# Rounded and rest passes of the side-by-side projections in runs instead of in turn, and some letters of the stage orders moved

## The chip, the cores and the metric

One core of one Trainium2 chip runs the whole program. The metric is the time of one execution on the device, in microseconds (us). Three runs of the kernel before gave 851.22, 853.45 and 853.88 us; their median, 853.45 us, is the time before. A separate execution was profiled: 852.3 us in all, of which 850.5 us lie between the first and the last instruction (the span).

The engines are named as in the profile: PE multiplies matrices (PEld is its loading of the stationary operand), ACT, DVE and POOL work on vectors, SP issues the transfers (DMA) of weights.

## The reference

A two-layer encoder of 256 tokens by 1024 channels, in float32, cut to what matters here:

```python
for i in range(2):
    h = rms_norm(x, norm_mix[i])
    x = x + (even_mixer if i == 0 else odd_mixer)(h, ...)   # Hyena + latent attention | differential attention
    x = x + cross_attention(rms_norm(x, norm_cross[i]), mem_n, xa_wq[i], xa_wkv[i], xa_wo[i])
    x = x + sq_relu_mlp(rms_norm(x, norm_mlp[i]), mlp_up[i], mlp_down[i])
return rms_norm(x, final_norm)
# cross_attention: q = h @ wq; k, v = split(mem_n @ wkv); 4 heads of 256, 256 memory tokens; softmax(q k^T) v @ wo
# sq_relu_mlp: square(relu(h @ w_up)) @ w_down, 1024 -> 4096 -> 1024
```

## The kernel before

PE takes float32 as it is (slowly) or in a rounded form, float32r. The kernel splits each operand into a rounded value and the rest that rounding left, both float32r: `weight` (lines 90 to 107) loads 512 KB of a weight into `wraw` by a DMA of SP's queue, ACT writes the rounded part `whi` and DVE the rest `wlo`. There are four `wraw` buffers and six pairs of `whi`/`wlo`, so ACT and DVE prepare weights ahead and then wait until PE gives a pair back. A product is three passes: rounded by rounded, rounded by rest, rest by rounded (`mm3`, lines 113 to 117).

For the queries of the cross-attention, the up-projections of the MLP and the keys of the first cross-attention the passes are laid side by side (`side_by_side`, line 223). The activations hold the rounded 256 tokens and the rests of the 256 tokens next to each other in one tile `both` (`t` in the rows, `memB` for the memory tokens). One matmul of 512 columns multiplies `whi` by both halves (line 229, here the rounded pass), and one of 256 columns adds `wlo` by the rounded half (line 225, here the rest pass). Both add into one PSUM bank of 512 columns; at the end `joined` (line 242) has ACT copy the second half and DVE add the first. Each pair of passes takes one 128 by 128 block of the weight. `proj_w4` (line 234) covers four banks of 128 output channels: the weight comes in four quarters, and a quarter holds two blocks for each bank, 8 pairs; a projection has 32. `mem_k2` (line 294) covers two banks with a weight in two halves of four blocks for each bank, 16 pairs. There are 4 query projections (two in each cross-attention), 16 up-projections and 4 key projections of the `mem_k2` kind. In each bank a rounded pass and its rest pass stand in turn; only in the last pair of a bank the rest comes first, so that the rounded pass ends the sum over the whole bank.

PSUM has eight banks, given out in turn by name: four `h`, three `b`, one `f`. A projection can write a bank only after ACT and DVE have read what stood in it.

The strings `ORDER_EVEN`, `ORDER_CROSS` and `ORDER_ODD` (lines 30 to 35) give the order in which the stages of a mixer or a cross-attention are written down; `run` (line 124) calls one function for each letter. A scheduler then merges the instructions of neighbouring stages into one fixed list for each engine, and each engine works through its list in order. In the cross-attention Q is the projection of two heads' queries, K keys, V values, S scores and softmax of a head, B the transposed probabilities times the values, W the output projection. In the even mixer G is the second layer of the filter features, R the transposed queries, S and O scores and outputs of a latent-attention head, F filters, T transposes to tokens, P the spectrum, W the first half of the output projection. In the odd mixer A is scores and softmax, B the product with the values and C the norm of a head.

`Gained` (line 185) transposes the residual as it comes out of the previous output projection and splits it for the next one; the last quarter of it is left over and done by `flush` after the first weight quarter of the next projection.

Of the kernel before, what the change touches and what calls it, by code (L numbers as in the profile page):

```python
# [17 lines left out]
P = 128  # L18
D = 1024
# [5 lines left out]
C1 = 6.28125  # L25
C2 = float(np.float32(TWO_PI - C1))
C3 = float(np.float32(TWO_PI - C1 - C2))
PI_LO = 3.1415925

ORDER_EVEN = "X J H0 L U K G R S0 D H1 F0 S1 T0 S2 S3 P0 O0 O1 O2 H2 S4 O3 H3 T1 F1 S5 S6 O4 O5 Y S7 H4 P1 H5 O6 O7 M W"  # L30
ORDER_CROSS = [
    "Q0 V0 K0 K1 S0 B0 K2 S1 Q1 K3 S2 W0 V2 B1 S3 B2 B3 W1",
    "K0 K1 Q0 V0 S0 S1 K2 B0 Q1 K3 S2 V1 B1 V2 B2 W0 V3 S3 B3 W1",
]
ORDER_ODD = "Q2 Q0 Q1 A0 A1 B0 A2 C0 B1 B2 Q4 C1 C2 Q3 A3 A4 Q5 A5 B3 B4 C3 A6 C4 B5 B6 C5 A7 W0 W1 C6 B7 C7"


@with_exitstack
def tile_encoder(ctx: ExitStack, tc: tile.TileContext, a: dict, out: bass.AP):
    nc = tc.nc  # L40
# [3 lines left out]
    def T(pool, shape, dt, tag, **kw):  # L44
        count[0] += 1
        return pool.tile(shape, dt, tag=tag, name=f"{tag}_{count[0]}", **kw)
# [10 lines left out]
    def hb():  # L57
        return T(ps, [P, 512], F32, "h", bufs=4)

    def wk():  # L60
        return T(ps, [P, 512], F32, "b", bufs=3)
# [7 lines left out]
    def hilo():  # L69
        z = t16().rearrange("p (k s n) -> p k s n", k=8, s=2)  # L70
        return z[:, :, 0, :], z[:, :, 1, :], z
# [10 lines left out]
    def h2(n=512):  # L82
        return T(ep, [P, 512], F32, "h2", bufs=8)[:, :n]
# [4 lines left out]
    def v3(t, k):  # L88
        return t.rearrange("p (k n) -> p k n", k=k)

    def weight(src, cols=1024, side=False, gi=None, nk=2, raw=None):
        p_, x, nr, nw = (rp, "f", 2, 2) if side else (wp, "w", 4, 6)
        if raw is None:
            raw = T(p_, [P, 1024], F32, x + "raw", bufs=nr)[:, :cols]
            nc.sync.dma_start(raw, src)
        hi = T(p_, [P, 1024], F32R, x + "hi", bufs=nw)[:, :cols]
        lo = T(p_, [P, 1024], F32R, x + "lo", bufs=nw)[:, :cols]
        if gi is None:
            split(hi, lo, raw)
            return hi, lo  # L100
        gi, k0 = gi
        for k in range(nk):
            g = gcol[:, gi, k0 + k:k0 + k + 1]
            h_, l_, r_ = (v3(z, nk)[:, k, :] for z in (hi, lo, raw))
            nc.scalar.activation(h_, r_, AF.Identity, bias=zero, scale=g)  # L105
            nc.vector.scalar_tensor_tensor(l_, r_, g, h_.bitcast(F32), op0=ALU.mult, op1=ALU.subtract)  # L106
        return hi, lo

    def split(hi, lo, src):
        nc.scalar.copy(hi, src)  # L110
        nc.vector.tensor_tensor(lo, src, hi.bitcast(F32), op=ALU.subtract)  # L111
# [12 lines left out]
    def run(order, **ops):  # L124
        for w in order.split():
            ops[w[0]](*(int(n) for n in w[1:]))
# [19 lines left out]
    h = hilo()[:2]  # L146
    lat_all = t16(F32)
    lat_raw = [lat_all[:, i * 832:(i + 1) * 832] for i in range(4)]
    for c in range(2):
        for t in range(2):  # L150
            cs = slice(c * 512, (c + 1) * 512)
# [68 lines left out]
            if mid is not None and q == at:  # L220
                mid()

    def side_by_side(b, w, both, kk):
        def low():
            nc.tensor.matmul(b[:, :256], w[1], both[:, kk, 0, :], start=False, stop=False)  # L225

        if kk == 7:
            low()
        nc.tensor.matmul(v3(b, 2), w[0], both[:, kk], start=kk == 0, stop=kk == 7)  # L229
        if kk < 7:  # L230
            low()

    def proj_w4(h, src, banks, gi, mid=None):
        both = h[2]
        for i in range(4):
            wh, wl = (v3(z, 2) for z in weight(src[i], gi=(gi, 2 * i)))
            for c in range(4):
                for k in range(2):
                    side_by_side(banks[c], [z[:, k, c * P:(c + 1) * P] for z in (wh, wl)], both, 2 * i + k)
            if mid is not None and i == 0:  # L240
                mid()

    def joined(b0, b1):
        y = v3(T(cur["jp"], [P, 512], F32, "join", bufs=3), 2)
        for i, b in enumerate((b0, b1)):
            nc.scalar.copy(y[:, i, :], b[:, 256:])
            nc.vector.tensor_tensor(y[:, i, :], b[:, :256], y[:, i, :], op=ALU.add)
        return y
# [35 lines left out]
    memB = T(cst, [P, 8, 2, 256], F32R, "memB")  # L284
# [9 lines left out]
    def mem_k2(l, u):  # L294
        bs = [wk(), wk()]
        for i in range(2):
            wh, wl = (v3(z, 4) for z in weight(a["xa_wk"][l, u, i]))
            for c in range(2):
                for k in range(4):
                    side_by_side(bs[c], [z[:, k, c * P:(c + 1) * P] for z in (wh, wl)], memB, 4 * i + k)  # L300
        y = joined(*bs)
        k = [T(rp, [P, 2, 256], F32R, f"kTm{i}", bufs=2) for i in range(2)]
        split(k[0], k[1], y)
        return k
# [177 lines left out]
    R = T(ep, [P, 256], F32, "rrow")  # L482
# [213 lines left out]
    def mla_proj():  # L696
        hs["b"] = [[wk(), wk()], [wk(), fl()]]
        proj_down(catm, (0, 1, 2, 3), a["w_out_ev"], (4, 5, 6, 7), hs["b"], True)

    run(ORDER_EVEN, S=mla_s, O=mla_o, H=hy_chunk, F=filters, T=toks, P=spec, Y=conv0, W=mla_proj, M=mem_T,  # L700
        J=lat_proj, L=latents, U=queries, K=keys_values, R=queries_T, D=tables, G=features_2, X=rope_gains)
    ys, banks = hs["y"], hs["b"]
    cat = hilo()[:2]
    for u in range(2):
        b = hb()
        b4 = b.rearrange("p (c t n) -> p c t n", c=2, t=2)
        for c in range(2):
            cs = slice((2 * u + c) * P, (2 * u + c + 1) * P)
# [3 lines left out]
        z = v3(h2(), 2)  # L712
# [12 lines left out]
    def cross(l, cur_):  # L725
# [11 lines left out]
        def qproj(u):  # L737
            bs = [hb() for _ in range(4)]
            proj_w4(h, a["xa_wq"][l, u], bs, 2 + l, lambda: cur_.flush(wk))
            for i in range(2):  # L740
                y = joined(*bs[2 * i:2 * i + 2])
                qTs[2 * u + i] = [v3(T(cur["jp"], [P, 512], F32R, "qT", bufs=8), 2) for _ in range(2)]
                split(*qTs[2 * u + i], y)
# [3 lines left out]
        def mk(hd):  # L747
            ks[hd] = mem_k(l, hd) if l else mem_k2(l, hd)
# [39 lines left out]
    def mlp(l, cur_, nxt):  # L788
# [10 lines left out]
        def up(f):  # L799
            uh = T(mp, [P, 4, 256], F32R, "uh", bufs=2)  # L800
            ul = T(mp, [P, 4, 256], F32R, "ul", bufs=2)
            bs = [hb() for _ in range(4)] if f == 0 else [wk(), wk(), wk(), fl()]
            proj_w4(h, a["mlp_up"][l, f], bs, 4 + l, lambda: cur_.flush(wk))
            if f == 1:
                banks.extend([hb(), hb()] for t in range(2))
            for j in range(2):
                y = joined(*bs[2 * j:2 * j + 2])
                sq = v3(t2(), 2)
                nc.vector.scalar_tensor_tensor(sq, y, 0.0, y, op0=ALU.max, op1=ALU.mult)
                split(uh[:, 2 * j:2 * j + 2, :], ul[:, 2 * j:2 * j + 2, :], sq)  # L810
            return uh, ul
# [36 lines left out]
    h, ssq = cur_.h, cur_.ssq  # L848
# [109 lines left out]

    run(ORDER_ODD, Q=qkv, A=od_a, B=od_b, C=od_c, W=od_out)
    nxt = Gained()  # L960
# [139 lines left out]
```

## Time and profile before

| | |
|---|---|
| runs | 851.22, 853.45, 853.88 us |
| profiled execution | 852.3 us, span 850.5 us |
| PE busy | 829.4 us, 98% of the span, 4514 matmuls |
| DVE, ACT, POOL busy | 586.6, 508.2, 19.5 us |
| moved by DMA | 138.89 MB, mean 163 GB/s |
| TensorE clock granted | 0.997 of full speed (mean) |

A matmul's duration in the profile contains time in which it lies over its neighbours (a matmul of 512 columns is given about 398 ns, while its successor starts 227 to 241 ns after it). What a matmul costs in a row of matmuls is therefore read from the distance of the starts, not from the duration. An idle time in brackets names the instruction that ended it.

### The profile page before, as it was taken

What the parts mean: (1) busy time and instruction counts of PE and PEld (TensorE: products, weight loads), DVE (VectorE), ACT (ScalarE), POOL (GpSimd) and SP (SyncE); (2) the same over time, 40 slices, a digit from 0 to 9 for tenths busy, and PEclk for the clock granted to TensorE, in tenths of its full rate; (3) what the DMA queues carried; (4) which work ended last, traced back from release to release, by engine and by line L of the source; (5) the groups of instructions that cost most, each with busy time, mean ns of one, the idle gap of its engine ahead of it and who ended that gap; (6) DMA issues with size and microseconds to landing.
All of it is one profiled execution on the core that took longest, in us unless ns stands there. A gap on an engine that the chain in (4) does not pass through costs nothing.

```text
span 850.5 us, 12079 instructions
## 1 busy us (share of the span) xinstructions
PE 829.4 (98%) x4514; PEld 695.0 (82%) x4514; DVE 586.6 (69%) x940; ACT 508.2 (60%) x883; POOL 19.5 (2%) x51
## 2 busy tenths in 40 slices
PE   6999999999999999999999999999999999999996
PEld 5867587788888888888888788889998888888885
DVE  4978796876658666666668888677654776666663
ACT  5896464766447555555567667666543755555542
POOL 0010000000000000000000010100000000000000
PEclk9999999999999999999999999999999999999998
DMA  7660317765527666666647416245522566656641
GB/s 275 199 207 19 121 36 263 236 209 159 170 68 218 202 187 190 192 191 186 196 132 226 153 66 198 75 145 178 159 90 100 168 201 189 189 191 184 191 125 50
DMA packets 39519, 138.89 MB, mean 163 GB/s; under 512 B 4515, under 2 KB 5155, under 8 KB 39461
## 3 DMA queue, kind: packets, MB, share of 16 engines
q1 hardware_dynamic: 39460, 138.13, 51.6%
q8 instruction: 35, 0.57, 0.3%
q14 instruction: 24, 0.19, 0.1%
HBM read 137.06 MB, written 1.05 MB: 162 GB/s over the span
## 4 chain that ended last, share of the span: by engine, by line
PE 79%; issue 11%; ACT 4%; DVE 2%; DMA 2%; POOL 1%; SPq 0%; POOLq 0%; ACTq 0%; DVEq 0%
PE h L115 12%; PE h L116 12%; PE h L117 12%; PE b L229 11%; PE b L225 5%; PE h L229 4%; PE f L229 3%; PE b L115 2%; PE h L225 2%; PE b L116 2%; PE b L117 2%; PE f L115 2%; PE f L116 2%; PE f L117 2%; PE f L225 2%
## 5 line engine op out<-in xcount | busy, mean ns | idle before, releaser
L111 DVE TENSOR_TENSOR wlo<-wraw,whi 128x1024 fp32r<-128x1024 f32 (+1 forms) x127 | 153.9, 1218 | 100.9 <-ACT whi L110 100.3
L110 ACT CAST whi<-wraw 128x1024 fp32r<-128x1024 f32 (+1 forms) x127 | 132.5, 1048 | 124.0 <-PE f L229 42.7
L105 ACT ACTIVATE whi<-wraw,zero,cpack 128x512 fp32r<-128x512 f32 x208 | 160.0, 811 | 62.6 <-PE h L117 20.3
L106 DVE SCALAR_TENSOR_TENSOR wlo<-wraw,cpack,whi 128x512 fp32r<-128x512 f32 x208 | 150.3, 749 | 42.8 <-ACT whi L105 42.6
L229 PE MATMUL b<-t,whi 128*128 128x512 f32 x336 | 119.5, 398 | 0.0
L117 PE MATMUL h<-whi,ul 128*128 128x512 f32 x256 | 99.9, 390 | 0.0
L115 PE MATMUL h<-whi,uh 128*128 128x512 f32 x256 | 99.6, 389 | 0.0
L116 PE MATMUL h<-wlo,uh 128*128 128x512 f32 x256 | 99.6, 389 | 0.0
L225 PE MATMUL b<-t,wlo 128*128 128x256 f32 x336 | 87.3, 280 | 0.0
L115 PE MATMUL h<-whi,t 128*128 128x512 f32 x192 | 76.8, 401 | 0.0
L116 PE MATMUL h<-wlo,t 128*128 128x512 f32 x192 | 76.5, 399 | 0.0
L117 PE MATMUL h<-whi,t 128*128 128x512 f32 x192 | 76.0, 397 | 0.0
L229 PEld LDWEIGHTS b<-t,whi 128*128 128x128 f32 x336 | 61.1, 188 | 12.2
L229 PE MATMUL h<-t,whi 128*128 128x512 f32 x192 | 67.9, 400 | 1.4 <-DVE t L111 1.4
L225 PEld LDWEIGHTS b<-t,wlo 128*128 128x128 f32 x336 | 63.4, 189 | 3.7
L116 PEld LDWEIGHTS h<-wlo,uh 128*128 128x128 f32 x256 | 48.0, 188 | 10.1
L117 PEld LDWEIGHTS h<-whi,ul 128*128 128x128 f32 x256 | 48.1, 188 | 9.9
L115 PEld LDWEIGHTS h<-whi,uh 128*128 128x128 f32 x256 | 48.1, 188 | 9.3
L225 PE MATMUL h<-t,wlo 128*128 128x256 f32 x192 | 50.0, 281 | 0.0
L229 PE MATMUL f<-t,whi 128*128 128x512 f32 x112 | 42.7, 398 | 0.0
L117 PEld LDWEIGHTS h<-whi,t 128*128 128x128 f32 x192 | 36.1, 188 | 7.2 <-DVE t L111 0.2
L115 PEld LDWEIGHTS h<-whi,t 128*128 128x128 f32 x192 | 36.1, 188 | 7.0
(325 smaller groups left out, 1633.1 us busy)
## 6 DMA issues: line engine op xcount, KB each, us to landing
wraw<-in_mlp_up_dram SPq DMA_DIRECT2D x64, 512.0 KB, 4.2
wraw<-in_mlp_down_dram SPq DMA_DIRECT2D x64, 512.0 KB, 4.3
wraw<-in_od_w_qkv_dram SPq DMA_DIRECT2D x24, 512.0 KB, 4.3
wraw<-in_xa_wq_dram SPq DMA_DIRECT2D x16, 512.0 KB, 4.1
wraw<-in_xa_wo_dram SPq DMA_DIRECT2D x16, 512.0 KB, 4.2
wraw<-in_w_hy_dram SPq DMA_DIRECT2D x12, 512.0 KB, 4.0
wraw<-in_w_out_ev_dram SPq DMA_DIRECT2D x8, 512.0 KB, 4.4
wraw<-in_xa_wv_dram SPq DMA_DIRECT2D x8, 512.0 KB, 5.4
```

What stands on the lines that cost most here:

```text
L105: nc.scalar.activation(h_, r_, AF.Identity, bias=zero, scale=g)
L106: nc.vector.scalar_tensor_tensor(l_, r_, g, h_.bitcast(F32), op0=ALU.mult, op1=ALU.subtract)
L110: nc.scalar.copy(hi, src)
L111: nc.vector.tensor_tensor(lo, src, hi.bitcast(F32), op=ALU.subtract)
L115: nc.tensor.matmul(o, lh, rh, start=first, stop=False)
L116: nc.tensor.matmul(o, lh, rl, start=False, stop=False)
L117: return nc.tensor.matmul(o, ll, rh, start=False, stop=last)
L225: nc.tensor.matmul(b[:, :256], w[1], both[:, kk, 0, :], start=False, stop=False)
L229: nc.tensor.matmul(v3(b, 2), w[0], both[:, kk], start=kk == 0, stop=kk == 7)
```

## The change

The diff, cut to its core (two orders of three are left out here: in the even mixer G moves from before R to behind S0, P0 and S3 change places, and so do S5 and S6; in the odd mixer A5 and B3 change places, and B5 and B6):

```diff
 ORDER_CROSS = [
-    "Q0 V0 K0 K1 S0 B0 K2 S1 Q1 K3 S2 W0 V2 B1 S3 B2 B3 W1",
+    "Q0 V0 K0 K2 S0 K1 B0 V2 S1 Q1 K3 S2 B1 W0 S3 B2 B3 W1",
...
-    def side_by_side(b, w, both, kk):
...
+    def side_by_side(banks, w, both, k0):
+        wh, wl = w
+        nk = wh.shape[1]
+        last = k0 + nk == 8
+
+        def high(c, k):
+            nc.tensor.matmul(v3(banks[c], 2), wh[:, k, c * P:(c + 1) * P], both[:, k0 + k],
+                             start=k0 + k == 0, stop=last and k == nk - 1)
+
+        def low(c, k):
+            nc.tensor.matmul(banks[c][:, :256], wl[:, k, c * P:(c + 1) * P], both[:, k0 + k, 0, :],
+                             start=False, stop=False)
+
+        every = range(len(banks))
+        for cs in [(c,) for c in every] if last else [every]:
+            for one in (low, high) if k0 // nk % 2 else (high, low):
+                for c in cs:
+                    for k in range(nk):
+                        one(c, k)
...
     def proj_w4(h, src, banks, gi, mid=None):
-        both = h[2]
         for i in range(4):
-            wh, wl = (v3(z, 2) for z in weight(src[i], gi=(gi, 2 * i)))
-            for c in range(4):
-                for k in range(2):
-                    side_by_side(banks[c], [z[:, k, c * P:(c + 1) * P] for z in (wh, wl)], both, 2 * i + k)
+            w = [v3(z, 2) for z in weight(src[i], gi=(gi, 2 * i))]
+            side_by_side(banks, w, h[2], 2 * i)
             if mid is not None and i == 0:
                 mid()
```

A four-bank projection now does its first quarter as 8 rounded passes over all banks and then 8 rest passes, the second as 8 rests and 8 rounded, the third as 8 rounded and 8 rests, and the last bank by bank, two rests and two rounded each. With the neighbours joined that is a run of 8, runs of 16, 16 and 8, and then runs of 2. A two-bank key projection has 8 rounded, 8 rests, and then bank by bank four rests and four rounded. No matmul is added or taken away; line 229 keeps its number for the rounded pass, and the rest pass is now line 233.

PE, the first query projection of the first cross-attention, before (`h_1503` to `h_1506` are its four banks, `whi_1509` and `wlo_1510` its first weight quarter, `t_297` the activations, `b_1531` the bank of `flush`):

```order
L229 MATMUL h_1503<-t_297_1388,whi_1509 128x512
L225 MATMUL h_1503<-t_297_1388,wlo_1510 128x256
...
L229 MATMUL h_1504<-t_297_1388,whi_1509 128x512
L225 MATMUL h_1504<-t_297_1388,wlo_1510 128x256
...
L229 MATMUL h_1506<-t_297_1388,whi_1509 128x512
L225 MATMUL h_1506<-t_297_1388,wlo_1510 128x256
...
L181 MATMUL b_1531<-cpack_70,t_296_1385 128x128 x4
L229 MATMUL h_1503<-t_297_1388,whi_1540 128x512
```

The same place on PE after the change:

```order
L229 MATMUL h_1503<-t_297_1388,whi_1509 128x512 x2
L229 MATMUL h_1504<-t_297_1388,whi_1509 128x512 x2
L229 MATMUL h_1505<-t_297_1388,whi_1509 128x512 x2
L229 MATMUL h_1506<-t_297_1388,whi_1509 128x512 x2
L233 MATMUL h_1503<-t_297_1388,wlo_1510 128x256 x2
L233 MATMUL h_1504<-t_297_1388,wlo_1510 128x256 x2
L233 MATMUL h_1505<-t_297_1388,wlo_1510 128x256 x2
L233 MATMUL h_1506<-t_297_1388,wlo_1510 128x256 x2
L181 MATMUL b_1531<-cpack_70,t_296_1385 128x128 x4
L233 MATMUL h_1503<-t_297_1388,wlo_1541 128x256 x2
```

The fourth bank, written first after 12 passes of both kinds before, is now written after 6 rounded ones.

PE, the first key projection (K0) of the first cross-attention, before, with the last row of the values (V0) ahead of it (`b_1708` and `b_1709` are the two banks of K0, `b_1629` one of V0):

```order
L117 MATMUL b_1629<-whi_1686,memB_91 128x512
L229 MATMUL b_1708<-memB_91,whi_1712 128x512
L225 MATMUL b_1708<-memB_91,wlo_1713 128x256
...
L229 MATMUL b_1709<-memB_91,whi_1712 128x512
L225 MATMUL b_1709<-memB_91,wlo_1713 128x256
```

The same place on PE after the change:

```order
L117 MATMUL b_1629<-whi_1686,memB_91 128x512
L229 MATMUL b_1708<-memB_91,whi_1712 128x512 x4
L229 MATMUL b_1709<-memB_91,whi_1712 128x512 x4
L233 MATMUL b_1708<-memB_91,wlo_1713 128x256 x4
L233 MATMUL b_1709<-memB_91,wlo_1713 128x256 x4
L233 MATMUL b_1708<-memB_91,wlo_1735 128x256 x4
```

The second bank follows four rounded passes now, where four rounded and four rest passes stood ahead of it.

PE, the transposed probabilities of head 1 (L455, a part of B1) in the first cross-attention, before (`b_2183` is a bank of the values V2, `b_2271` the bank of B1's product, `b_2286` that of the scores S3):

```order
L117 MATMUL b_2183<-whi_2240,memB_91 128x512
L455 MATMUL b_2264<-cpack_70,t_401_1937 128x128 x4
L115 MATMUL b_2271<-t_468_2262,vp_355_1702 128x256
L115 MATMUL b_2286<-kTm_435_2114,qT_2059 128x256
L116 MATMUL b_2286<-kTm_436_2115,qT_2059 128x256
```

The same step on PE after the change (L459 are the transposes, `b_2231` is the bank of the product, `h_2246` and `h_2247` are banks of W0):

```order
L117 MATMUL b_2198<-kTm_378_1815,qT_2131 128x256
L459 MATMUL b_2224<-cpack_70,t_417_2017 128x128 x4
L115 MATMUL h_2246<-whi_2252,t_317_1499 128x512
...
L116 MATMUL h_2247<-wlo_2259,t_317_1499 128x512
L115 MATMUL b_2231<-t_458_2222,vp_355_1702 128x256
```

Between the transposes and the product that uses them stand 17 matmuls of the output projection W0; before, nothing stood there. V2 stands behind B0's transposes and ahead of S1.

## Rows read from the trace of the kernel before

**Rows 1.** The page: busy time; granted clock in 40 slices; chain that ended last.

```profile
PE 829.4 (98%) x4514; PEld 695.0 (82%) x4514; DVE 586.6 (69%) x940; ACT 508.2 (60%) x883; POOL 19.5 (2%) x51
...
PEclk9999999999999999999999999999999999999998
...
PE 79%; issue 11%; ACT 4%; DVE 2%; DMA 2%; POOL 1%; SPq 0%; POOLq 0%; ACTq 0%; DVEq 0%
```

**Rows 2.** Groups by line and shape, line 229 (columns as page part 5).

```profile
L229 PE MATMUL b<-t,whi 128*128 128x512 f32 x336 | 119.5, 398 | 0.0
...
L229 PE MATMUL h<-t,whi 128*128 128x512 f32 x192 | 67.9, 400 | 1.4 <-DVE t L111 1.4
...
L229 PE MATMUL f<-t,whi 128*128 128x512 f32 x112 | 42.7, 398 | 0.0
...
L229 PE MATMUL b<-memB,whi 128*128 128x512 f32 x64 | 22.6, 398 | 0.1
```

**Rows 3.** Timeline of PE, one up-projection: start, duration in us, then engine and instruction.

```profile
698.77 0.39 PE L229 MATMUL b<-t,whi 128*128 128x512 f32 x1
...
707.25 0.40 PE L229 MATMUL b<-t,whi 128*128 128x512 f32 x1
...
710.04 0.39 PE L115 MATMUL h<-whi,uh 128*128 128x512 f32 x1
```

**Rows 4.** Timeline, end of V0: first and last of 14 matmuls of 512 columns.

```profile
168.62 0.39 PE L116 MATMUL b<-wlo,memB 128*128 128x512 f32 x1
...
171.57 0.39 PE L117 MATMUL b<-whi,memB 128*128 128x512 f32 x1
```

**Rows 5.** Timeline, second-layer keys: first and last of 48 matmuls of 256 columns.

```profile
565.90 0.28 PE L115 MATMUL f<-memB,fhi 128*128 128x256 f32 x1
...
571.54 0.28 PE L117 MATMUL f<-memB,flo 128*128 128x256 f32 x1
```

**Rows 6.** Timeline, first query projection: what its third quarter waits for.

```profile
147.83 0.39 PE L229 MATMUL h<-t,whi 128*128 128x512 f32 x1
...
149.15 0.68 DVE L111 TENSOR_TENSOR t<-h,t 128x512 fp32r<-128x512 f32 x1
...
153.27 0.57 ACT L110 CAST t<-b 128x512 fp32r<-128x512 f32 x1
...
155.23 0.49 PE L229 MATMUL h<-t,whi 128*128 128x512 f32 x1 [1.12 <-DVE t L111]
```

**Rows 7.** Timeline, K0: first pass, DVE reading V0's banks, second bank.

```profile
171.79 0.39 PE L229 MATMUL b<-memB,whi 128*128 128x512 f32 x1
...
172.69 1.28 DVE L111 TENSOR_TENSOR vp<-b,vp 128x512 fp32r<-128x512 f32 x2
...
173.43 0.50 PE L229 MATMUL b<-memB,whi 128*128 128x512 f32 x1
```

**Rows 8.** Timeline, B1 of the first cross-attention.

```profile
228.79 0.60 PE L455 MATMUL b<-cpack,t 128*128 128x128 f32 x4
...
229.47 0.59 ACT L110 CAST t<-b 128x512 fp32r<-128x512 f32 x1
...
230.12 0.39 PE L115 MATMUL b<-t,vp 128*128 128x256 f32 x1 [0.73 <-ACT t L110]
```

**Rows 9.** Timeline, end of the odd mixer and start of the second cross-attention's queries.

```profile
563.13 0.28 PE L117 MATMUL f<-memB,flo 128*128 128x256 f32 x1
...
563.68 0.50 PE L229 MATMUL h<-t,whi 128*128 128x512 f32 x1 [0.28 <-DVE t L111]
```

**Rows 10.** Timeline, the latent attention's part of the even output projection.

```profile
124.98 0.50 PE L116 MATMUL f<-wlo,catm 128*128 128x512 f32 x1 [0.75 <-DVE wlo L111]
```

**Rows 11.** Timeline, start of the second layer's first up-projection.

```profile
664.95 0.40 PE L229 MATMUL h<-t,whi 128*128 128x512 f32 x1
...
665.15 0.69 DVE L278 TENSOR_TENSOR t<-h,t 128x512 f32<-128x512 f32 x1 [0.39 <-PE h L117]
```

**Rows 12.** Timeline, even mixer: PE's first filter matmuls.

```profile
51.32 3.67 PE L385 MATMUL h<-t,aT 128*128 128x512 f32 x8
```

More of the change, by code (lines that the diff above doesn't have):

```diff
@@ L28 @@
 PI_LO = 3.1415925
-ORDER_EVEN = "X J H0 L U K G R S0 D H1 F0 S1 T0 S2 S3 P0 O0 O1 O2 H2 S4 O3 H3 T1 F1 S5 S6 O4 O5 Y S7 H4 P1 H5 O6 O7 M W"
+ORDER_EVEN = "X J H0 L U K R S0 G D H1 F0 S1 T0 S2 P0 S3 O0 O1 O2 H2 S4 O3 H3 T1 F1 S6 S5 O4 O5 Y S7 H4 P1 H5 O6 O7 M W"
 ORDER_CROSS = [
-    "Q0 V0 K0 K1 S0 B0 K2 S1 Q1 K3 S2 W0 V2 B1 S3 B2 B3 W1",
+    "Q0 V0 K0 K2 S0 K1 B0 V2 S1 Q1 K3 S2 B1 W0 S3 B2 B3 W1",
     "K0 K1 Q0 V0 S0 S1 K2 B0 Q1 K3 S2 V1 B1 V2 B2 W0 V3 S3 B3 W1",
 ]
-ORDER_ODD = "Q2 Q0 Q1 A0 A1 B0 A2 C0 B1 B2 Q4 C1 C2 Q3 A3 A4 Q5 A5 B3 B4 C3 A6 C4 B5 B6 C5 A7 W0 W1 C6 B7 C7"
+ORDER_ODD = "Q2 Q0 Q1 A0 A1 B0 A2 C0 B1 B2 Q4 C1 C2 Q3 A3 A4 Q5 B3 A5 B4 C3 A6 C4 B6 B5 C5 A7 W0 W1 C6 B7 C7"
 @with_exitstack
@@ L221, in proj_xs @@
                 mid()
-    def side_by_side(b, w, both, kk):
[L224 to L231, printed above, removed]
+    def side_by_side(banks, w, both, k0):
[14 more added lines that the diff above has]
+                        one(c, k)
     def proj_w4(h, src, banks, gi, mid=None):
-        both = h[2]
         for i in range(4):
-            wh, wl = (v3(z, 2) for z in weight(src[i], gi=(gi, 2 * i)))
-            for c in range(4):
-                for k in range(2):
-                    side_by_side(banks[c], [z[:, k, c * P:(c + 1) * P] for z in (wh, wl)], both, 2 * i + k)
+            w = [v3(z, 2) for z in weight(src[i], gi=(gi, 2 * i))]
+            side_by_side(banks, w, h[2], 2 * i)
             if mid is not None and i == 0:
@@ L296, in mem_k2 @@
         for i in range(2):
[L297 to L300, printed above, removed]
+            side_by_side(bs, [v3(z, 4) for z in weight(a["xa_wk"][l, u, i])], memB, 4 * i)
         y = joined(*bs)
```

## The prediction

> **What bounds the kernel now.** I read the page first: PE is busy for 829.4 of 850.5 us, and the chain that ended last is PE for 79% and "issue" for 11% (an engine waiting for nothing that the profile shows); ACT, DVE and DMA together hold 8% [rows 1]. So the time is the sum of the distances between the starts of PE's matmuls, and only two things can change it: that distance, and PE's few waits. Next I read the grouped lines for how many matmuls the edit touches: line 229 has 336, 192, 112 and 64 matmuls [rows 2], together 704 rounded passes, each with one rest pass. Then the timeline for their distances, and last the timeline around PE's waits.
>
> **The pace of passes in turn and in runs.** In an up-projection the first three weight quarters are 24 pairs in turn. They take from 698.77 to 707.25 us, 8.48 us, that is 353.3 ns a pair; the last quarter, where the order is rounded, rest, rest, rounded, takes from 707.25 to 710.04 us for 8 pairs, 348.8 ns a pair [rows 3]. So the distance depends on what stands next to what: with two changes of kind for each pair it is 353.3, with one 348.8. For runs of one kind the nearest rows are other matmuls of the same shapes: 512 columns follow each other every 226.9 ns (168.62 to 171.57 us, 13 steps) [rows 4], 256 columns every 120.0 ns (565.90 to 571.54 us, 47 steps) [rows 5]. A pair in runs would then cost 346.9 ns, 6.4 ns less than in turn.
>
> How many pairs gain: the last quarter of a four-bank projection has two rests and two rounded passes in turn after the change as well, so it gains nothing. The other 24 pairs go into runs, in 20 such projections 480. Of the 16 pairs in each of the four two-bank key projections I count 12, since their second half keeps runs of only four; 48 more. 528 times 6.4 ns is 3.4 us. Three changes of kind remain in the first three quarters; at half of the 6.4 ns each, 20 x 3 x 3.2 ns, they take back 0.2. The term is **-3.2 us**.
>
> Its bounds: if runs get no further than the two-and-two order of the last quarter (348.8), 528 x 4.5 ns is 2.4 us. If every change of kind costs 4.5 ns, as the step from 353.3 to 348.8 would have it, a pair without any costs 344.3: 528 x 9.0 less 60 x 4.5 ns is 4.5 us. I take 6.4, because its two rows are long runs of exactly these shapes.
>
> The granted clock doesn't enter: it stood at the upper of its two levels, 2.4 GHz, in all slices but the last [rows 1].
>
> The Trainium skill ("TensorE: Matmul & The Clock Gate", section "Back-to-back issue gap") gives a distance of columns through 2.4 GHz plus about 2.5 ns, whatever stands ahead. By it, as an estimate, a pair would cost 325 ns in either order, and this term would be zero. The trace disagrees, since 8 pairs take different times in two orders [rows 3]; what would happen if the order didn't matter is the second rival below.
>
> **The first query projection.** Its third quarter starts at 155.23 after a wait of 1.12 us for the split of the part that `flush` transposes; ACT begins that split only at 153.27, behind other work of its list [rows 6]. ACT's list has the same order there after the change, so what PE gains in the first two quarters (16 pairs, 0.1 us) is waited away: **+0.1**. The fourth bank is now wanted after 6 rounded passes, 1.4 us after the start, where 6 pairs took 2.1 us before; DVE still reads it until 149.83 [rows 6], 2.0 us after the start at 147.83. That stall of some 0.6 us also falls into the 1.12 us and costs nothing as long as that wait stands; without this cover it would cost 0.6. Behind PE's wait stand flush's transposes, which ACT doesn't want before 153.27.
>
> **K0.** PE starts it at 171.79; its second bank is one that V0 filled, and DVE reads it in the first of two operations from 172.69 on; PE got it at 173.43 [rows 7]. By then all 8 passes into the first bank were done. Now only four rounded ones stand ahead (0.9 us, until 172.70), and PE waits about 0.7 us in place of 0.2. The four rests (4 x 0.12) that used to fill the time come later: **+0.45**. Below that it can be nothing, if DVE is there earlier; above, 0.7.
>
> The same earlier wish for a bank arises in every projection. The nearest row for the rest is the second layer's first up-projection: start 664.95, DVE's last reading from 665.15 for 0.69, so until 665.84; the fourth bank is wanted at 664.95 + 1.36 = 666.31 [rows 11]. There 0.5 us remain, so I count nothing; between two up-projections a whole down-projection lies.
>
> **B1 of the first cross-attention.** PE's transposes start at 228.79 and take 0.44; then PE waits for ACT, which begins its copy at 229.47, and goes on at 230.12 [rows 8]: 0.9 us with nothing between. After the change 17 matmuls of W0 stand there, 17 x 0.227 = 3.9 us, which covers ACT's 0.59 and DVE's split. V2 now stands ahead of S1, and B0's product is covered by 8 rounded passes of the next query projection (1.8 us). **-0.9**; at worst none, if B0's transposes now wait in its stead.
>
> **End of the odd mixer.** From 563.13 to 563.68 PE stands for 0.55 us where 0.12 would do, for DVE's split ahead of the second cross-attention's queries [rows 9]. After the change 25 matmuls of the second layer's keys and values stand between (25 x 0.12 = 3.0 us). **-0.4**. The wait moves nowhere else that I see: those matmuls were due anyway.
>
> **The even mixer.** Its letters move several things of about one us. For gain: the rest of a weight for which PE waits 0.75 us until 124.98 [rows 10] stood in DVE's list behind four splits of the memory tokens; it now stands ahead of them, and the wait could go. For loss: the queries' copies now come ahead of G's sine on ACT, and PE's first filter matmuls, which began at 51.32 [rows 12], now stand ahead of the scores of head 1 and want G's result some 1.5 us earlier; S0 follows right on the transposes whose copies it needs. I bound this part by -0.75 (the one wait gone, nothing new) and +1.5 (the wait stays and the filters stand for those 1.5 us), and take **0**, since the wait that may go and one that may come are of the same order and no row tells which is the larger.
>
> **Sum.** -3.2 + 0.1 + 0.45 - 0.9 - 0.4 + 0 = -3.95 us on the profiled 852.3, which gives 848.35, a factor of 0.9954. The profiled execution lies 0.13% below the median of the runs shown, so on 853.45 it is **849.5 us**.
>
> **Rivals.**
> 1. The runs pay more, and the even mixer's wait goes: -4.5 for the pace instead of -3.2, and -0.75: 849.5 - 2.05 = 847.4. For it: the step between the two orders in rows 3. Against: rows 4 and 5 show 346.9 in runs that have no change of kind at all.
> 2. The pace doesn't follow the order. Then only the waits move: 0.45 - 0.9 - 0.4 = -0.85, so 852.6, no change. For it: rows 4 and 5 are of other operands than these passes. Against: rows 3. The page of the Trainium skill cited above speaks for this one. A variant: the pace is won, but the mixers give 1.5 us and B1's 0.9 back, 851.9.
> 3. Slower: the banks. A run of 8 rounded passes wants the last bank 0.7 us earlier in all 24 projections. If ACT and DVE had just been in time in the others, as in K0 (0.5 us lost), 20 more times 0.5 is 10 us against the 3.2 won: 859.5. It decides from about 12 such projections on. For it: K0 and the first query projection in rows 6 and 7. Against: 0.5 us to spare in rows 11, and banks that lie idle for a whole down-projection.
>
> **How the numbers follow.** 0.3% of the median is 2.6 us, about what can be told from no change; faster is below 850.9, slower above 856.0. The forecast has 0.55, with a range of its own of 847.8 to 851.2; rival 1 has 0.15; rival 2 with its variant 0.23; rival 3 has 0.07. Of the forecast 0.51 lies below 850.9; with rival 1 faster gets 0.66. Same gets 0.04 + 0.23 = 0.27, slower 0.07. The range leaves out rival 3 and the ends of the others: 846.5 to 852.8.
>
> **What would show it.** In the trace after, an up-projection from its first rounded pass to the first matmul of the down-projection should take 11.1 us in place of 11.27 [rows 3]; rounded passes in a run 227 ns apart, rests 120. K0 should stand about 0.7 us ahead of its second bank. No wait should follow the transposes of B1, and the second cross-attention's queries should start without one. PE's waits in the even mixer should sum to what they were. It would be wrong if rounded passes in a run stood 233 ns or more apart, if PE stood in many projections after the sixth rounded pass, or if the first cross-attention began more than 1.5 us later than before.

## The result, and the profile after

Four runs of the kernel after gave 846.05 to 846.86 us, median 846.43; four of the kernel before beside them 853.66. The ratio is 0.9921, with a 95% interval from 0.9904 to 0.9938: 6.7 us less (5.3 to 8.2). The forecast was 849.5, a gain of 4.0 us. The sign was right. The median lies 0.07 us below the range of 846.5 to 852.8; by the ratio, on the 853.45 us that the forecast started from, the time is 846.7 us, just inside it. The gain is 1.7 times the forecast, and, as the experiments show, its largest single part comes from the even mixer, which the forecast had at 0. Further runs of the kernel before, beside the experiments, have medians of 852.98 to 853.16.

The page of the kernel after; its span is 844.7 us, its time 846.44:

```profile
PE 824.9 (98%) x4514; PEld 695.0 (82%) x4514; DVE 589.7 (70%) x940; ACT 511.1 (61%) x883; POOL 19.3 (2%) x51
...
PEclk9999999999999999999999999999999999999998
...
PE 81%; issue 11%; ACT 4%; DVE 1%; POOL 1%; DMA 0%; SPq 0%; POOLq 0%; ACTq 0%; DVEq 0%
```

PE still bounds it: the same 4514 matmuls at the same clock [rows 1], 4.5 us less busy. ACT, DVE and DMA hold 5% of the chain instead of 8.

The groups of line 229 after, by shape:

```profile
L229 PE MATMUL b<-t,whi 128*128 128x512 f32 x336 | 90.7, 392 | 0.0
...
L229 PE MATMUL h<-t,whi 128*128 128x512 f32 x192 | 50.9, 394 | 0.4 <-DVE t L111 0.4
...
L229 PE MATMUL f<-t,whi 128*128 128x512 f32 x112 | 34.6, 390 | 0.0
L229 PE MATMUL b<-memB,whi 128*128 128x512 f32 x64 | 16.6, 394 | 0.0
```

A lesson in reading: against [rows 2] the busy sums fall by 60 us in all, though the kernel gained 7. The time in which passes of one group lie over each other is counted once: in a run neighbours are of one group, in turn they belong to two. Only distances of starts tell the pace. The idle time ahead of the queries fell from 1.4 to 0.4 us.

An up-projection after, at the place of [rows 3] (x6 stands for six passes in one row): start, end of the third quarter, first matmul of the down-projection:

```profile
693.77 1.52 PE L229 MATMUL b<-t,whi 128*128 128x512 f32 x6
...
702.10 0.40 PE L233 MATMUL b<-t,wlo 128*128 128x256 f32 x2
...
704.89 0.39 PE L115 MATMUL h<-whi,uh 128*128 128x512 f32 x1
```

24 pairs take 8.33 us where they took 8.48, and the whole 11.12 instead of 11.27. The rounded passes of a run stand 227 ns apart, the rests 120, as in [rows 4, 5].

K0 after, at the place of [rows 7]: first passes on PE, DVE reading V0's banks:

```profile
169.74 2.08 PE L229 MATMUL b<-memB,whi 128*128 128x512 f32 x8
```
```profile
169.88 1.37 DVE L111 TENSOR_TENSOR vp<-b,vp 128x512 fp32r<-128x512 f32 x2 [0.31 <-ACT vp L110]
```

DVE reads the banks 0.14 us after K0's start, not 0.90 as before; PE gets the second bank with a delay of 0.1. The forecast stall of 0.7 is not there.

B1 after, at the place of [rows 8]: ACT's copy of the transposes, and the first product:

```profile
224.54 0.58 ACT L110 CAST t<-b 128x512 fp32r<-128x512 f32 x1
...
225.18 0.39 PE L115 MATMUL b<-t,vp 128*128 128x256 f32 x1
```

No wait is left. Nor has the second cross-attention's first query pass one [rows 9]:

```profile
564.98 1.32 PE L229 MATMUL h<-t,whi 128*128 128x512 f32 x5
```

The wait of [rows 10] in the even output projection is gone as well, while others grew, among them this one ahead of the filters, where there was none [rows 12]. It is a wait for a load and not, as the prediction had it, for G's result. The query projection's wait of [rows 6] shrank to 0.42 us:

```profile
49.84 1.52 PE L389 MATMUL h<-t,aT 128*128 128x512 f32 x3 [0.79 <-DMA t<-in_hy_w_dram]
```
```profile
153.15 2.14 PE L229 MATMUL h<-t,whi 128*128 128x512 f32 x8 [0.42 <-DVE t L111]
```

### The profile page after: what moved, and what is told of

Read it like the earlier page. It is cut to its first block, busy times and chain, and to the rows that moved or that the text cites. A ratio compares the mean times of both kernels' runs of the same rounds, so it can differ in the third digit from the quotient of the medians.

```text
span 844.7 us, 12071 instructions
## 1 busy us (share of the span) xinstructions
PE 824.9 (98%) x4514; PEld 695.0 (82%) x4514; DVE 589.7 (70%) x940; ACT 511.1 (61%) x883; POOL 19.3 (2%) x51
## 2 busy tenths in 40 slices
DMA packets 39518, 138.89 MB, mean 164 GB/s; under 512 B 4514, under 2 KB 5154, under 8 KB 39460
## 4 chain that ended last, share of the span: by engine, by line
PE 81%; issue 11%; ACT 4%; DVE 1%; POOL 1%; DMA 0%; SPq 0%; POOLq 0%; ACTq 0%; DVEq 0%
PE h L115 12%; PE h L117 12%; PE h L116 12%; PE b L229 11%; PE b L233 6%; PE h L229 5%; PE f L229 3%; PE b L115 3%; PE b L116 3%; PE b L117 3%; PE h L233 2%; PE f L115 2%; PE f L116 2%; PE f L117 2%; PE f L233 2%
## 5 line engine op out<-in xcount | busy, mean ns | idle before, releaser
L105 ACT ACTIVATE whi<-wraw,zero,cpack 128x512 fp32r<-128x512 f32 x208 | 158.3, 810 | 54.0 <-PE h L117 20.8
L229 PE MATMUL b<-t,whi 128*128 128x512 f32 x336 | 90.7, 392 | 0.0
L229 PEld LDWEIGHTS b<-t,whi 128*128 128x128 f32 x336 | 59.3, 189 | 9.0
L233 PEld LDWEIGHTS b<-t,wlo 128*128 128x128 f32 x336 | 49.8, 190 | 4.7
L233 PE MATMUL b<-t,wlo 128*128 128x256 f32 x336 | 53.5, 282 | 0.0
L229 PE MATMUL h<-t,whi 128*128 128x512 f32 x192 | 50.9, 394 | 0.4 <-DVE t L111 0.4
L116 PEld LDWEIGHTS h<-wlo,t 128*128 128x128 f32 x192 | 36.1, 188 | 6.7
L229 PEld LDWEIGHTS h<-t,whi 128*128 128x128 f32 x192 | 33.6, 188 | 6.3 <-DVE t L111 1.3
```

What stands on the lines that cost most here:

```text
L116: nc.tensor.matmul(o, lh, rl, start=False, stop=False)
L229: nc.tensor.matmul(v3(banks[c], 2), wh[:, k, c * P:(c + 1) * P], both[:, k0 + k], start=k0 + k == 0, stop=last and k == nk - 1)
L233: nc.tensor.matmul(banks[c][:, :256], wl[:, k, c * P:(c + 1) * P], both[:, k0 + k, 0, :], start=False, stop=False)
```

## The experiments

Each was timed against the kernel before; of two only the trace was read.

**The pass order alone**

```diff
 (the kernel after)
-ORDER_EVEN, ORDER_CROSS[0], ORDER_ODD as after
+ORDER_EVEN, ORDER_CROSS[0], ORDER_ODD as before
```

> The new pass order alone, with the letters of before. By the forecast: -3.2 us for the pace, +0.1 at the first query projection, +0.45 at K0, together -2.65 us (ratio 0.9969). By the trace of after, where an up-projection lost 0.147 us and K0 did not wait: 20 x 0.147 = -2.9 us (ratio 0.9966), and the waits of before at the even output projection (0.96 us until its first rest pass), at B1 (0.93 us) and at the end of the odd mixer (0.43 us) all still there. Rival, the letters brought most of the gain: the ratio is above 0.998.

Measured: 851.87 us, ratio 0.9977 (0.9965 to 0.9989), 2.0 us less; twelve runs lie between 848.6 and 852.7. In the profiled one (852.67 us, the slowest of the twelve) everything behind the first query projection is 2.5 us shorter than before, but the projection starts 1.9 us later and itself takes 14.06 us instead of 13.08. Its start, from the timeline, PE first, then ACT and DVE:

```profile
149.73 1.53 PE L229 MATMUL h<-t,whi 128*128 128x512 f32 x6
...
152.75 0.50 PE L229 MATMUL h<-t,whi 128*128 128x512 f32 x1 [1.49 <-DVE t L111]
```
```profile
149.79 1.05 ACT L110 CAST fhi<-fraw 128x1024 fp32r<-128x1024 f32 x1 [4.41 <-DMA fraw<-in_xa_wk_dram]
150.74 0.58 ACT L110 CAST t<-h 128x512 fp32r<-128x512 f32 x1
```
```profile
152.01 0.68 DVE L111 TENSOR_TENSOR t<-h,t 128x512 fp32r<-128x512 f32 x1
```

After six rounded passes PE wants the fourth bank. DVE reads it at 152.01. ACT's copy of it comes only at 150.74, behind ACT's rounding of a key weight, for whose transfer ACT had waited 4.41 us; and DVE takes the rest of that same weight first (from 150.87, for 1.23 us). The stall is real, 1.5 us, and a late load sets it.

**The letters alone**

```diff
 (the kernel before, passes in turn)
-ORDER_EVEN, ORDER_CROSS[0], ORDER_ODD as before
+ORDER_EVEN, ORDER_CROSS[0], ORDER_ODD as after
```

> The moved letters alone, with the passes in turn. By the forecast: -0.9 at B1, -0.4 at the end of the odd mixer, 0 in the even mixer, together -1.3 us (ratio 0.9985). By the trace of after, which gives the even mixer about -0.9 besides: -2.2 us (0.9974). Rival, most of the change lies in the letters: -4 us or more (0.995). The up-projections take 11.27 us as before in all cases.

Measured: 848.92 us, 0.9954 (0.9941 to 0.9967), 3.9 us less. The letters bring more than the passes; the two, 2.0 and 3.9, make up the whole within the intervals.

**The even mixer's letters alone**

```diff
-ORDER_EVEN = "... K G R S0 D ... S2 S3 P0 ... S5 S6 ..."
+ORDER_EVEN = "... K R S0 G D ... S2 P0 S3 ... S6 S5 ..."
```

> The letters of the even mixer alone. By the forecast 0 us (ratio 1.000): one wait of about 1 us goes, another of about 1 us comes ahead of the filter matmuls. By the trace of after -0.9 us (0.999). Rival, the whole excess over the forecast sits here: -2.5 us (0.997). The wait for wlo in the even output projection (0.96 us in the trace of before) is gone, and a wait of about 1 us stands ahead of the first filter matmuls, in all cases.

Measured: 849.90 us, 0.9967 (0.9955 to 0.9979), 2.8 us less. So the forecast's 0 for this part was wrong, and the rival is right: the excess over the forecast, 2.8 us, is as large as what this part gains.

**The first cross-attention's letters alone**

```diff
-    "Q0 V0 K0 K1 S0 B0 K2 S1 Q1 K3 S2 W0 V2 B1 S3 B2 B3 W1",
+    "Q0 V0 K0 K2 S0 K1 B0 V2 S1 Q1 K3 S2 B1 W0 S3 B2 B3 W1",
```

> The letters of the first cross-attention alone. By the forecast -0.9 us (ratio 0.9989): the wait behind B1's transposes goes and nothing else changes. Rival: another wait takes its place and the ratio is 1.000; or V2 ahead of S1 covers more than B1's wait and it is 0.998.

Measured: 852.69 us, 0.9995 (0.9986 to 1.0003): too small to be told from none. In its trace the stretch from the first scores to the first up-projection takes 71.22 us instead of 72.00, 0.8 less, and the wait behind B1 is gone; that agrees with -0.9.

**Eight orders of the passes, two up-projections each**

```diff
-            side_by_side(banks, w, h[2], 2 * i)
+            side_by_side(banks, w, h[2], 2 * i, seen[0] % 8)   # order by the projection's number
...
```

> The 16 up-projections do the first three weight quarters (24 pairs) in eight patterns, two each; the time from the first rounded pass of each to the first pass of its last quarter is read. Theory A, each change between rounded and rest costs (forecast, 3.2 ns a change over a floor of 346.9 ns a pair): in turn 8.48 us; in turn with the banks changing at every pair 8.48; two and two in a bank 8.40; fours 8.36; eights and sixteens as in after 8.33; in turn with the rest pass one pair late 8.48; eights with the bank changing at every pass 8.33. Theory B, in turn costs only where the banks change (the keys of before, four pairs in a bank, took 349 ns a pair in turn against 353.3 with two pairs in a bank): in turn with the banks changing at every pair above 8.55, eights with the bank changing at every pass above 8.40, and the key projection that changes banks at every pair above 5.65 us in place of 5.58.

PE's timeline, first pass of a projection and first pass of its last quarter: in turn; in turn with the banks changing at every pair; two and two; eights with the bank changing at every pass.

```profile
760.74 0.39 PE L229 MATMUL b<-t,whi 128*128 128x512 f32 x1
769.21 0.40 PE L233 MATMUL b<-t,wlo 128*128 128x256 f32 x2
...
782.92 0.39 PE L229 MATMUL b<-t,whi 128*128 128x512 f32 x1
791.39 0.40 PE L233 MATMUL b<-t,wlo 128*128 128x256 f32 x2
...
805.09 0.62 PE L229 MATMUL b<-t,whi 128*128 128x512 f32 x2
813.44 0.40 PE L233 MATMUL b<-t,wlo 128*128 128x256 f32 x2
...
351.89 0.84 PE L229 MATMUL b<-t,whi 128*128 128x512 f32 x3
360.24 0.40 PE L233 MATMUL b<-t,wlo 128*128 128x256 f32 x2
```

8.47, 8.47, 8.35 and 8.35 us; fours took 8.39, the order of after 8.34, and the eighth order, twos whose kinds are swapped from bank to bank, 8.39. Theory A falls: two and two, with a change for every pair, is as quick as eights, and fours are slower than twos. Theory B falls too: banks that change twice as often in turn cost nothing more. The rests one pair late, which are in turn as well, took 8.45. What remains is a plain fact of these up-projections: strict turn is the slow order, and runs of two or more lie between 8.34 and 8.39. (The key projection that changes banks at every pair took 5.64 us, near what B wanted; but in the trace of the letters alone the keys in turn, with four pairs in a bank, take 5.63 to 5.66 us as well.)

**Four pairs in a bank, in turn**

```diff
-        for i in range(4):
+        for qs in ((0, 1), (2,), (3,)):        # the first two quarters' blocks of a bank together
...
```

> The kernel before, in turn, with the first two weight quarters of a four-bank projection taken together, so that four pairs stand in one bank before the next (two before); third and last quarter as before. Read: 16 pairs of the first two quarters, 8 of the third. Theory, in turn is slow only where the banks change every second pair or oftener: 16 x 347.6 = 5.56 us, then 8 x 353.3 = 2.83 us. Rival, it lies in something else by which the up-projections differ from the keys (how the weight blocks lie in their tile): 16 x 353.3 = 5.65 us, then 2.83 us.

Two up-projections of this one kernel, first pass and first matmul behind the 16 pairs:

```profile
666.33 0.40 PE L229 MATMUL h<-t,whi 128*128 128x512 f32 x1
...
671.88 0.60 PE L181 MATMUL b<-cpack,t 128*128 128x128 f32 x4
...
700.17 0.39 PE L229 MATMUL b<-t,whi 128*128 128x512 f32 x1
...
705.81 0.40 PE L229 MATMUL b<-t,whi 128*128 128x512 f32 x1
```

5.55 us in one, 347 ns a pair, and 5.64 in the other, 352.5, with the same order. So the theory and its rival both miss: a pair in turn keeps one of two paces. What decides which was not found; the number of pairs in a bank isn't it. The two rows differ in the names of the banks, `h` and `b`, but that alone isn't it either: the second key projection, in turn on two `b` banks, took 5.58 us in the trace of before and 5.63 in that of the load buffers below.

**S5 and S6 alone**

```diff
-ORDER_EVEN = "... F1 S5 S6 O4 ..."
+ORDER_EVEN = "... F1 S6 S5 O4 ..."
```

> Of the kernel before only S5 and S6 of the even mixer change places. Theory from the even letters' run (-3.3 us): this exchange puts the rest of one even output weight ahead of the splits of the memory tokens on DVE, which gives its load buffer back early, so the weights of the first cross-attention arrive earlier: -2 to -3 us (ratio 0.9965 to 0.9977), wait for wlo in the even output projection gone, and the query weights' loads begin more than 1 us earlier before the first query projection. Rival, by the forecast's own bound, that one wait alone: -0.75 to -1 us (0.999). Rival, the gain belongs to G behind S0: 1.000.

Measured: 850.72 us, 0.9975 (0.9965 to 0.9984), 2.1 us less. One exchange of two letters brings most of the even mixer's gain. Where it does so, the trace shows in part. PE's rest pass of [rows 10] starts without a wait, and the even output projection, from its first to its last matmul, takes 52.49 us (from 80.66) where it took 53.58 (from 80.83), 1.1 less. But the wait in the query projection is 1.12 us, as in [rows 6], and from the end of the output projection to the end of the kernel nothing is gained (716.3 us, 716.1 before). The rest pass, the projection's last matmul and the query projection's wait in this kernel, and the last matmul in before:

```profile
123.84 0.48 PE L116 MATMUL f<-wlo,catm 128*128 128x512 f32 x1
...
133.15 0.39 PE L117 MATMUL b<-whi,catm 128*128 128x512 f32 x1
...
154.39 0.49 PE L229 MATMUL h<-t,whi 128*128 128x512 f32 x1 [1.12 <-DVE t L111]
```
```profile
134.41 0.40 PE L117 MATMUL f<-whi,catm 128*128 128x512 f32 x1
```

This execution is the slowest of the nine (851.21 us). Of the 2.1 us it shows 1.1; the rival's 0.75 to 1 lies outside the interval (1.4 to 3.0), and where the rest lies is not shown.

The exchange also moves the lists of DVE and of SP's queue, which are the same at this place in this kernel and in after. The kernel before: two rests of even output weights on DVE; the loads; and SP's longest wait between 90 and 130 us (sum, times, longest):

```profile
123.71 1.22 DVE L111 TENSOR_TENSOR wlo<-wraw,whi 128x1024 fp32r<-128x1024 f32 x1
...
126.02 1.22 DVE L111 TENSOR_TENSOR wlo<-wraw,whi 128x1024 fp32r<-128x1024 f32 x1
```
```profile
123.70 0.33 SPq L136 DMA_DIRECT2D t<-in_x_dram  x1
124.99 0.33 SPq L95 DMA_DIRECT2D wraw<-in_w_out_ev_dram  x1
...
127.30 0.33 SPq L95 DMA_DIRECT2D wraw<-in_w_out_ev_dram  x1
130.02 6.09 SPq L95 DMA_DIRECT2D wraw<-in_xa_wq_dram  x4
```
```profile
SPq L136 <- PE b L688: 29.3, 1, 29.3
```

The kernel after, the same:

```profile
117.78 1.22 DVE L111 TENSOR_TENSOR wlo<-wraw,whi 128x1024 fp32r<-128x1024 f32 x1
...
121.61 1.21 DVE L111 TENSOR_TENSOR wlo<-wraw,whi 128x1024 fp32r<-128x1024 f32 x1
```
```profile
119.06 4.16 SPq L95 DMA_DIRECT2D wraw<-in_w_out_ev_dram  x2
...
128.65 4.30 SPq L95 DMA_DIRECT2D wraw<-in_xa_wq_dram  x4
```

In before SP's list has the load of a residual tile (line 136) ahead of the last two output weights, and it waits 29.3 us for the transposes of the memory tokens (line 688) to give that tile back; everything behind it waits along. Then each weight begins when a rest is done and gives its `wraw` buffer back (123.71 + 1.22 = 124.93, and 124.99). In after the two weights stand ahead of the residual tile, and the rests come 4 to 6 us earlier (117.78 + 1.22 = 119.00, and 119.06). So the exchange moved two lists besides PE's; the rows of windows below show the transfers.

**Load buffers of their own, letters as before**

```diff
...
+            if src is a["w_out_ev"] and nxt is not None and k in (2, 3):
+                own = T(wp, [P, 1024], F32, "oraw", bufs=2)
+                nc.sync.dma_start(own, src[k])
+            ws.append(weight(src[k], raw=own))
```

> The kernel before, in which the last two weights of the even output projection have load buffers of their own and are loaded long before; on PE, DVE and ACT the even mixer's lists stand as before, PE's wait for wlo included. Theory, the S5/S6 exchange gained mainly by the loads of the query weights: they now begin more than 2 us earlier, PE's waits ahead of and in the first query projection (0.63 and 1.28 us in the trace of before) shrink, and the median falls by 1 to 2 us (ratio 0.9977 to 0.9988). Rival, it gained by the wait for wlo and the shorter way through DVE's list: 0.9995 to 1.0005, with the wait of 0.96 us still there.

Measured: 850.68 us, 0.9974 (0.9964 to 0.9984), 2.2 us less, though no letter was moved and the wait for `wlo` is still there. The two loads are now issued at 22.66 us. PE's waits in it between 120 and 157 us (sum, times, longest):

```profile
PE f L116 <- DVE wlo L111: 0.7, 1, 0.7
PE h L181 <- DVE t L284: 0.6, 1, 0.6
```

The query projection's wait of 1.12 us [rows 6] is gone, and the projection takes 11.89 us instead of 13.08. The trace is 2.4 us shorter than that of before; the other 1.2 us lie in the first 16 us, ahead of the moved loads, and say nothing about them. The stretch from 119 to 125 us in before, after and this kernel (the last figures are the clock, the share of the DMA engines and GB/s):

```profile
core 0: us, PE busy (x) PEld busy (x) DVE busy (x) ACT busy (x) POOL busy (x), PEclk, DMA share, GB/s
105.00:119.00 14.00, 14.00 (x112) 12.76 (x111) 13.30 (x27) 8.77 (x17) 0.00 (x0) 1.00 0.01 2
119.00:125.00 6.00, 5.25 (x47) 4.90 (x45) 5.27 (x13) 4.93 (x11) 0.00 (x0) 1.00 0.02 5
```
```profile
119.00:125.00 6.00, 6.00 (x46) 5.46 (x44) 5.77 (x13) 3.44 (x8) 0.00 (x0) 1.00 0.45 137
```
```profile
119.00:125.00 6.00, 5.25 (x41) 4.72 (x40) 5.33 (x13) 4.05 (x10) 0.00 (x0) 1.00 0.18 61
```

From 105 to 125 us the DMA engines of the kernel before stood still (1 and 2%): SP stood behind the residual tile, then at buffers whose rests were late. (In after they stood still as well, but only to 119 us.) Then they had to bring the output, query and value weights at once (0.79 busy, 273 GB/s from 125 to 148 us), and the query projection waited. In this kernel two weights less are due at that point, and that alone is worth 2.2 us (1.4 to 3.1). That the exchange of S5 and S6 gains as much does not show that it works by the loads. The two traces gain at different places: this one 1.2 us in the query projection, with the wait of [rows 10] left; that one 1.1 us where the wait of [rows 10] was, with the query projection's wait left. In the other traces with the exchange that wait is anything from none (G back, below) over 0.42 (after) to 1.14 us (eight orders). So what the loads have to do with the exchange's gain is open.

**A fifth buffer for all weights, before and after**

```diff
-        p_, x, nr, nw = (rp, "f", 2, 2) if side else (wp, "w", 4, 6)
+        p_, x, nr, nw = (rp, "f", 2, 2) if side else (wp, "w", 5, 6)
```

> The kernel before with a fifth load buffer (wraw) for the weights; letters and pass order as before, and on DVE the two rests of the even output weights still stand behind the splits of the memory tokens. Theory, the S5/S6 exchange gained because a load buffer came back early and the loads behind it started early: the fifth buffer does that without the exchange, the query weights of the first cross-attention land more than 1 us earlier before the first query projection, and the ratio is 0.9965 to 0.998 although PE's wait for wlo (0.96 us in the trace of before) stays. Rival, the gain was that wait and what followed from it in DVE's list, not the loads: 0.999 to 1.000.

> The kernel after with the fifth load buffer. If loads still hold back places of it (the fourth bank of the first query projection, 0.4 us, the transposes ahead of it, 1.15 us): 0.5 to 1.5 us faster than after (ratio to before 0.990 to 0.9915). Rival, the letters already gave the loads all the lead they need: as after, 0.992.

Measured: 852.02 us on before, 0.9992 (0.9981 to 1.0003); 847.57 on after, 0.9931 (0.9915 to 0.9946). No gain, and inconclusive on the cause, since SP's list moved: one weight more stands ahead of the load that the filters need, and on before PE waits 1.96 us for it at 50 us. On before PE's waits in the first query projection are gone there too.

**Two tries at a better version**

```diff
-ORDER_EVEN = "X J H0 L U K R S0 G D ..."
+ORDER_EVEN = "X J H0 L U K G R S0 D ..."
```

> The kernel after with G of the even mixer back ahead of R. Theory: G behind S0 only made the wait ahead of the first filter matmuls (about 0.95 us) and earned nothing against it; then this is 0.5 to 1 us faster than after (845.6, ratio to before 0.9910). Rival, G behind S0 gave the scores an earlier start that is worth the wait: as after, 846.4 (0.992). If G's place also held the early loads: 848 or more.

```diff
-        for cs in [(c,) for c in every] if last else [every]:
-            for one in (low, high) if k0 // nk % 2 else (high, low):
-                for c in cs:
...
+        for one in (low, high) if k0 // nk % 2 else (high, low):
+            for c in every:
...
```

> The kernel after with the last quarter of each projection in runs too, 8 rests and then 8 rounded passes over all banks. By the pace (348.8 ns a pair two and two, 346.9 in runs): 160 pairs x 1.9 ns, -0.3 us against after (846.1). Rival, the first banks end up to 0.9 us later, ACT and DVE square them later and the down-projection waits: 16 x 0.3 us or more, slower than after by 5 us.

Measured: G back 847.80 us, 0.9940 (0.9927 to 0.9952), against after's 846.43 rather a loss, though the intervals of the two ratios overlap; G behind the scores is worth its wait. In the trace with G back PE waits 0.8 and 0.4 us for ACT between 75 and 110 us, where after has neither. Last quarter in runs 846.40, 0.9925 (0.9912 to 0.9939), as after: that quarter took 2.80 us in place of 2.79. Nothing that was run beats the kernel after.

## Why the prediction was right in sign and short in size

- **Pace, -3.2.** The mechanism holds: 0.147 us for each of 16 up-projections, 2.35 us. The term was too large, because it counted the keys and the queries. The second key projection took 5.58 us in turn (5.63 in the trace of the letters alone) and takes 5.60 now: it already kept the quicker pace. The second query projection of the first cross-attention gained nothing that its stage shows: in the trace of the pass order alone the stretch from the first scores to the first up-projection takes 71.97 us instead of 72.00. The pass order alone gave 2.0 us (0.9 to 3.0). Rival 1's half on the pace (-4.5) is out, and so is rival 2. The formula cited for rival 2 (the Trainium skill, "TensorE: Matmul & The Clock Gate", section "Back-to-back issue gap") counts the columns alone, and the section gives it for a single matmul, not for a stream of them. Read as a rule by which the order ahead doesn't matter, it doesn't hold for these passes: 24 pairs took 8.47 us in one order and 8.35 in another within one run.
- **First query projection, +0.1.** The working took ACT's order for fixed times. The bank's freeing hangs on ACT's wait for a key weight's transfer: where that is late, the stall is 1.5 us (pass order alone); where the loads are early, as in after, the projection takes 12.58 us instead of 13.08. It came out at -0.5, for a reason that the forecast had not seen. This is also the one place where rival 3 showed itself.
- **K0, +0.45.** This failed: DVE was there 0.8 us earlier than [rows 7] gave. The delay in before came from a load again: ACT rounds a key weight, for which it waited 2.81 us, ahead of its copy of V0's banks, as these rows of before show. From K0 to the next keys the trace after is 0.3 shorter.

```profile
170.46 1.05 ACT L110 CAST whi<-wraw 128x1024 fp32r<-128x1024 f32 x1 [2.81 <-DMA wraw<-in_xa_wk_dram]
171.42 1.16 ACT L110 CAST vp<-b 128x512 fp32r<-128x512 f32 x2
```

- **B1, -0.9.** Right in the trace: 0.8 in the stage, the wait gone, none in its stead. The runs alone can't tell it from no gain.
- **End of the odd mixer, -0.4.** The wait is gone; in the trace of the letters alone the way from the odd mixer to the second layer's first down-projection is only 0.15 us shorter. The rest went into places not followed up.
- **The even mixer, 0, bounds -0.75 to +1.5.** This step failed, and it carries the miss: -2.8 us (-1.8 to -3.8). Both sides of its weighing were off. On the side of gain it priced the wait of [rows 10] at 0.75; the exchange of S5 and S6 that removes it gives 2.1 us (1.4 to 3.0), of which the trace shows 1.1 in that stage. On the side of loss it priced G's move at up to 1.5; the wait ahead of the filters did come, 0.79 us and for a load, but putting G back rather costs, 1.4 us by the medians. It also left out that the letters move SP's list and the load buffers. That the loads at this place are worth something is shown by the load buffers of their own (2.2 us by the runs; the trace has 1.2 of it in the query projection); that the exchange gains by the loads is not shown, and the rest of its gain stays open. Rival 1's "the even mixer's wait goes" named the place, not the size.

## What to carry to other kernels

An operation that is the last reader of a load buffer has two prices: who waits for its result, and which transfer waits for its buffer. Two changes that gain the same need not gain in the same way: compare their traces stage by stage, and leave out the stages that the edit doesn't touch, since the first 16 us of two traces here differ by 1.2 us. Where the DMA row of the page shows a stretch near zero ahead of one near full, look for the instruction that holds the buffers. Where the letters of stages move, read the queue of loads too: one that waits for its tile holds up all that stand behind it.

## What was not expected of the hardware

Passes of 512 and 256 columns in turn keep 353 ns a pair in most places and 347 in some, with the same instructions in the same order; in the slower pace of the run with four pairs in a bank the distances repeat every three pairs (232, 118, 241, 120, 236, 113 ns), in the quicker one every two (232, 118, 230, 113 ns). Runs of two and more kept 347 to 350. Why is open.

In the profiled run of the fifth buffer on before, PE's wait of 1.96 us was followed by a fall of the clock. The row of that stretch, and PE's first matmuls in it:

```profile
50.00:58.00 8.00, 6.04 (x13) 2.62 (x12) 6.12 (x12) 7.59 (x14) 1.70 (x4) 0.79 0.58 184
```
```profile
52.48 5.37 PE L385 MATMUL h<-t,aT 128*128 128x512 f32 x8 [1.96 <-DMA t<-in_hy_w_dram]
```

The mean granted clock is 0.79 here and 1.00 in the stretches on either side. The eight matmuls took 5.37 us instead of 3.67 [rows 12], four of them 0.85 us apart where the others stand 0.43 apart: these four ran at the lower of the two levels, 1.2 GHz, at a cost of 1.7 us. With the fifth buffer on after, a wait of 1.8 us at this place was followed by no such fall.
